# The down projection of an encoder layer as seven block products over 16 of its 22 key tiles

## The chip, the cores and the metric

The kernel runs on one core of a Trainium2 chip. The metric is the device time of one execution in microseconds. A core has TensorE (PE, matmuls, with its weight loads PEld), VectorE (DVE), ScalarE (ACT), GpSimd (POOL), SyncE (SP, which here issues nearly all transfers) and its DMA queues. Each engine takes its instructions strictly in the order of the program; between engines semaphores set the order.

## The reference

One post-norm encoder layer in float32 with 1024 tokens, 1024 features and 256 memory tokens: a token mixer (bidirectional mLSTM beside a neighbourhood attention), a cross-attention into `mem`, and a gated convolutional feed-forward part. The changed part is the last line of `conv_ffn` (D_FF is 2816, 22 tiles of 128):

```python
def conv_ffn(x, w_up, b_up, w_dw, b_dw, w_down, b_down):
    h = x @ w_up + b_up
    h = lax.conv_general_dilated(h, w_dw[:, None, :], window_strides=(1,), padding='SAME', ...
                                 feature_group_count=2 * D_FF) + b_dw
    g, u = jnp.split(h, 2, axis=-1)
    y = jax.nn.gelu(g, approximate=False) * u
    return y @ w_down + b_down
...
h = layer_norm(x, ln_in_w, ln_in_b)
h = layer_norm(DN_ALPHA * h + hybrid_mixer(h, ...), ln1_w, ln1_b)
h = layer_norm(DN_ALPHA * h + memory_xattn(h, mem, ...), ln2_w, ln2_b)
h = layer_norm(DN_ALPHA * h + conv_ffn(h, ...), ln3_w, ln3_b)
```

## The kernel before, in words

**Precision.** A product in float32 is made of three passes in float16. `split16(hi, lo, src, s)` (L202 to L204) scales a tensor by a power of two `s`: ACT writes the high part, DVE the remainder. `mm3` (L223 to L226) then issues three matmuls into one PSUM bank: high by high, high by low, low by high. `scale_of` (L185 to L191) takes the largest magnitude over a list of columns and makes the power of two; so a tensor's largest value must be known before its first split. To find it for w_down, the kernel reads the whole matrix once: `survey_down` (L1694) loads one key tile of 512 KB, and ACT takes its magnitude with a running sum into a column of `sums`.

**The stages**, in the order of the program, with the names that its tiles have in the profile: the input LayerNorm and the memory's keys and values; the token columns of the first projection (`tk`), with the cross-attention's `kv_gen` beside them; the block products of the mLSTM's q and k columns (`cu`, `units_gen`); the mLSTM chunks (`ml_gen`), between whose steps `mix` puts the remaining columns (`cl`, `col_gen`, 16 outputs of 24 matmuls each); the neighbourhood attention with the first output projection as fill; the cross-attention; the up projection in 22 units (`z`); the down projection (`dn`); the last LayerNorm. "The q/k columns" in this text are both the `cu` and the `cl` stage.

**Seven products for eight.** In the `cu` stage and in the units, a matrix product is cut into 2 x 2 blocks and done as seven block products rather than eight, with sums of blocks of the activations (`B11`, `T2`, ...) and of the weights (`A11`, `S2`, ...). In a unit, `prep` (L1549) makes the weight sums on POOL (four additions or subtractions of 128x512) and splits all on ACT and DVE; `take` (L1673) brings the banks into the tile C; `post` (L1648) does the convolution and the gate on ACT and DVE, writes the result y to memory (`y_d`, one tile of 128 channels x 1024 tokens per unit) and measures it. The other engines run at most two units ahead, since the buffers `ur` (raw weights) are two.

**The down projection** is plain. For each half of the output's columns (512 of 1024), for each of 8 token tiles, 22 key tiles x 3 passes go into one bank. y comes in pairs of tiles, is split once (`y_pair`, L1705) and stays; w_down comes in pairs too (`w_pair`, L1719), each half when it is wanted. The first 18 key tiles and the last 4 have scales of their own, because the last units end late; the two are joined by `ratio`. The first half's sums wait in `half0` (L1827 to L1855); the second half is followed tile by tile by the residual (POOL and DVE), the LayerNorm and the store (L1870 to L1889).

**What sets the order.** The program is written in the order of issue, apart from `mix` in the mLSTM stage, which lets a column product follow when the chunk has used up a given time. Generators (`kv_gen`, `units_gen`, `col_gen`, `prep`) give their steps when the surrounding loop calls them. All loads of raw weights and all stores share SP's list; a transfer whose source or target isn't ready holds everything behind it on SP. On chip, pools with a number of buffers (`bufs`) make a tile wait until the previous user of its buffer has been read for the last time.

## Time and profile before

| | us |
|---|---|
| median of the runs (3) | 1486.83 |
| lowest and highest | 1483.25, 1490.03 |
| the profiled execution, time | 1483.54 |
| the profiled execution, span | 1481.5 |
| PE busy in the span | 1432.5 (97%) |
| DVE, ACT, POOL busy | 1032.4 (70%), 820.2 (55%), 564.4 (38%) |
| moved by DMA | 208.61 MB, mean 141 GB/s |
| down projection, 1227.5 to 1474 | 246.5, of it PE 246.5 |
| q/k columns, 257 to 472 | 215, of it PE 212.2 |

How to read the lines that follow. A row of groups gives the source line, engine, operation, the tiles written and read, the shape of the first operand, the count, the busy time in all and the mean of one in ns, and the idle time of the engine just before these instructions with what ended it. A row of time order begins with the start and the duration in us; in brackets stands how long the engine had stood and for what. A row of stretches gives start and end, length, then busy time (and count) of PE, PEld, DVE, ACT and POOL, the granted TensorE clock (1.00 is full), the share of the 16 DMA engines that were busy, and GB/s.

### The profile page before, as it was taken

How to read it: one execution, taken by the hardware profiler on the slowest of the kernel's cores; microseconds unless marked ns; L12 is line 12 of the kernel's file. 1: busy time of each engine (PE TensorE's matmuls, PEld its weight loads, DVE VectorE, ACT ScalarE, POOL GpSimd, SP SyncE). 2: the span in 40 equal slices, each digit the busy share in tenths (PEclk: the TensorE clock that was granted, in tenths of full speed). 3: DMA queues.
4: the chain of work that ended last, by engine and by line, in shares of the span. 5: the costliest groups of instructions: out<-in, count | busy, mean ns of one | idle time of the engine just before them, and what ended most of it. 6: DMA issues, size and time to landing. Idle time of an engine off the chain costs nothing. (4 is left out here: it accounts for less than half of the span.)

```text
span 1481.5 us, 21508 instructions
## 1 busy us (share of the span) xinstructions
PE 1432.5 (97%) x7996; PEld 843.8 (57%) x7996; DVE 1032.4 (70%) x1946; ACT 820.2 (55%) x1385; POOL 564.4 (38%) x444
## 2 busy tenths in 40 slices
PE   8999899999999999999999799999999999999998
PEld 6998776456766777764444344444444444444444
DVE  7867866545777778588655958887778788717424
ACT  5765465564553677334546677777777866503001
POOL 5452356403324765055112534443444310300543
PEclk9999999999999999999999899999999999999999
DMA  8846654224654544743423323332333336703121
GB/s 305 311 182 196 187 197 149 79 50 136 161 146 158 199 137 155 272 128 63 99 53 114 126 90 128 128 133 108 123 132 116 136 125 237 255 29 109 48 71 58
DMA packets 116383, 208.61 MB, mean 141 GB/s; under 512 B 40627, under 2 KB 69555, under 8 KB 112950
## 3 DMA queue, kind: packets, MB, share of 16 engines
q1 hardware_dynamic: 115984, 206.47, 41.7%
q8 instruction: 63, 1.03, 0.3%
q0 software_dynamic: 144, 0.49, 0.2%
q14 instruction: 42, 0.34, 0.1%
q10 hardware_dynamic: 150, 0.27, 0.0%
HBM read 154.15 MB, written 45.15 MB: 135 GB/s over the span
## 5 line engine op out<-in xcount | busy, mean ns | idle before, releaser
L1567 POOL TENSOR_TENSOR wraw<-ur 128x512 f32<-128x512 f32 x22 | 45.8, 2082 | 205.2 <-issue 190.5
L225 PE MATMUL dn<-wlo,yp 128*128 128x512 f16 (+1 forms) x284 | 105.1, 370 | 0.0
L224 PE MATMUL dn<-whi,yp 128*128 128x512 f16 (+1 forms) x284 | 104.9, 370 | 0.0
L226 PE MATMUL dn<-whi,yp 128*128 128x512 f16 (+1 forms) x284 | 104.4, 370 | 0.0
L1655 DVE SCALAR_TENSOR_TENSOR cbuf<-C,wdw,cbuf 128x1024 f32<-128x1024 f32 x44 | 70.2, 1595 | 36.1 <-ACT cbuf L1654 36.0
L226 PEld LDWEIGHTS <-wlo 128*128 128x128 f16 x540 | 52.8, 98 | 56.5 <-DVE wlo L204 1.3
L225 PEld LDWEIGHTS <-whi 128*128 128x128 f16 x540 | 52.8, 98 | 54.7 <-issue 1.9
L224 PEld LDWEIGHTS <-whi 128*128 128x128 f16 x540 | 52.9, 98 | 53.2 <-ACT whi L203 0.3
L242 POOL TENSOR_TENSOR lnrs<-lnrs,mhalf 128x1 f32<-128x1 f32 x32 | 24.9, 777 | 133.7 <-DVE lnrs L241 96.2
L204 DVE SCALAR_TENSOR_TENSOR wlo<-wraw,us,whi 128x1024 f16<-128x1024 f32 (+1 forms) x48 | 62.7, 1323 | 18.6 <-ACT whi L203 18.6
L1656 DVE SCALAR_TENSOR_TENSOR cbuf<-C,wdw,cbuf 128x1024 f32<-128x1024 f32 x44 | 70.5, 1603 | 0.7
L252 ACT ACTIVATE r<-r,lnrs 128x1024 f32<-128x1024 f32 x19 | 23.5, 1238 | 81.4 <-DVE lnrs L251 81.3
L203 ACT ACTIVATE whi<-wraw,us 128x1024 f16<-128x1024 f32 (+1 forms) x48 | 51.1, 1102 | 15.5 <-DVE us L176 15.4
L225 PEld LDWEIGHTS <-yp 128*128 128x128 f16 x370 | 36.2, 98 | 39.9
L1654 ACT ACTIVATE cbuf<-C,bdw,wdw 128x1024 f32<-128x1024 f32 x44 | 54.2, 1234 | 8.6 <-DVE C L1692 8.1
L224 PEld LDWEIGHTS <-yp 128*128 128x128 f16 x370 | 36.2, 98 | 39.8
L226 PEld LDWEIGHTS <-yp 128*128 128x128 f16 x370 | 36.2, 98 | 39.7
L224 PE MATMUL tk<-whi,Bo 128*128 128x256 f16 (+1 forms) x192 | 52.6, 274 | 2.6 <-DVE stage L204 2.6
L225 PE MATMUL tk<-wlo,Be 128*128 128x256 f16 (+1 forms) x192 | 52.4, 274 | 0.8 <-DVE wlo L204 0.8
L224 PE MATMUL tk<-whi,Be 128*128 128x256 f16 (+1 forms) x192 | 52.5, 274 | 0.2 <-DVE stage L204 0.2
L226 PE MATMUL tk<-whi,Bo 128*128 128x256 f16 (+1 forms) x192 | 52.5, 274 | 0.0
L225 PE MATMUL tk<-wlo,Bo 128*128 128x256 f16 (+1 forms) x192 | 52.5, 274 | 0.0
(527 smaller groups left out, 4821.6 us busy)
## 6 DMA issues: line engine op xcount, KB each, us to landing
ur<-in_w_up_dram SPq DMA_DIRECT2D x22, 1024.0 KB
sv<-in_w_down_dram SPq DMA_DIRECT2D x22, 512.0 KB
y<-cbuf SPq DMA_DIRECT2D x22, 512.0 KB
ur<-y SPq DMA_DIRECT2D x11, 1024.0 KB
wraw<-in_w_down_dram SPq DMA_DIRECT2D x22, 512.0 KB
r<-h SPq DMA_DIRECT2D x11, 512.0 KB
wraw<-in_w_tok_dram SPq DMA_DIRECT2D x10, 512.0 KB
wr<-in_w_xk_dram SPq DMA_DIRECT2D x8, 512.0 KB
```

Source lines behind the costliest of these rows:

```text
L203: A.activation(hi, src, AF.Copy, scale=s)
L204: return V.scalar_tensor_tensor(lo, src, s, hi, op0=OP.mult, op1=OP.subtract)
L224: T.matmul(ps, lh, rh, start=first, stop=False, skip_group_check=skip)
L225: T.matmul(ps, lh, rl, start=False, stop=False, skip_group_check=skip)
L226: return T.matmul(ps, ll, rh, start=False, stop=last, skip_group_check=skip)
L242: G.tensor_tensor(rs[:, 0:1], rs[:, 0:1], mhalf[:, 0:1], OP.pow)
L252: A.activation(r, r, AF.Identity, scale=rs[:, 0:1], bias=rs[:, 1:2])
L1567: G.tensor_tensor(S1, A21, A22, OP.add)
L1654: A.activation(c, C[:, 1:SEQ + 1], AF.Identity, scale=wdw[:, 1, j:j + 1], bias=bdw[:, j:j + 1])
L1655: V.scalar_tensor_tensor(c, C[:, 0:SEQ], wdw[:, 0, j:j + 1], c, op0=OP.mult, op1=OP.add)
L1656: V.scalar_tensor_tensor(c, C[:, 2:SEQ + 2], wdw[:, 2, j:j + 1], c, op0=OP.mult, op1=OP.add)
```

## The change

Three parts, in the order of the program.

1. **The survey of w_down moves.** The 22 loads and ACT passes of `survey_down` leave the units and are issued in the token columns, one at each of 22 of the 32 steps, into two buffers `svd`.

2. **The weight forms are made early.** The 22 key tiles are numbered f. Of the first 16, tile i and tile i + 8 (i from 0 to 7) make a 2 x 2 block: two key halves by two column halves B11, B12, B21, B22. `wd_gen` loads both (1 MB, one buffer `draw`), and POOL makes T1 = B12 - B11, T2 = B22 - T1, T3 = B22 - B12 and T4 = B21 - T2, in place where it can. Seven forms are split (two buffers `dhl`) and stored to `wf_d`, 256 KB each. The last six key tiles are only split and stored (`wl_d`). The steps are called two at a time at each yield of `units_gen`, one at each yield of `ml_gen` (`with_prep`), and what is left runs before the attention.

3. **The down projection.** The 1024 tokens are cut by even (a = 0) and odd (a = 1) token tiles, the 16 keys into halves: A11, A12 (even), A21, A22 (odd). The seven products, each of 4 token tiles x 8 key tiles x 3 passes into four banks of 512 columns: A11·B11, A12·B21, A22·T4, S2·T2, S1·T1, S3·T3 and S4·B22, with S1 = A21 + A22, S2 = S1 - A11, S3 = A11 - A21, S4 = A12 - S2. `a_plain` reads one block's tiles of y again in rows of 512 B and splits them (128x2048); `a_sums` reads a pair of y tiles whole (1 MB) and makes S2 and S1, or S3 and S4, of it on DVE, then splits both. `b_load` reads the stored forms, on POOL's queue (the first one on SP's). `into` adds banks into the result C (128 x 8 x 1024), by a copy on ACT or an addition on DVE. The last six key tiles follow as plain products for both column halves, tile by tile, in the order of odd tiles and then even ones, and with them the LayerNorm. The scale of y now has exponent 12 rather than 14 for the first 16 tiles (sums of three blocks must fit), NG is 16, and the residual is added early, four tiles at a time (`rest`).

The arithmetic changes (sums of blocks in float32 before they are split); the result is the same function of the inputs.

```diff
@@ token columns
+                    def survey_down(i):
+
+                        t = w1.tile([128, D], F32, name="svd", tag="svd", bufs=2)
+                        S.dma_start(t, I["w_down"][i // 2, :, i % 2 * 1024:i % 2 * 1024 + 1024])
+                        A.activation(t, t, AF.Abs, accum_out=sums[:, NFF + i:NFF + i + 1])
+
                     for c in range(4):
                         w, ic = cw[2 + c]
                         for tt in range(NT):
+                            if 4 <= 8 * c + tt < 4 + NFF:
+                                survey_down(8 * c + tt - 4)
@@ q/k columns
+            FORMS = ("B11", "B21", "T4", "T2", "T1", "T3", "B22")
...
+            def wd_gen():
+
+                sd = scale_of(sums[:, NFF:2 * NFF], 12)[1]
+                scales["d"] = sd
+
+                def load(fs):
+                    raw = dp.tile([128, 2, 1024], F32, name="draw", tag="draw")
+                    for n, f in enumerate(fs):
+                        S.dma_start(raw[:, n], I["w_down"][f // 2, :, f % 2 * 1024:f % 2 * 1024 + 1024])
+                    return raw
+
+                def put(dst, src):
+                    hl = dp.tile([128, 2, 512], F16, name="dhl", tag="dhl", bufs=2)
+                    split16(hl[:, 0], hl[:, 1], src, sd)
+                    S.dma_start(dst, hl)
+
+                for i in range(8):
+                    raw = load((i, i + 8))
+                    T2 = dp.tile([128, 512], F32, name="dsum", tag="dsum")
+                    B11, B12, B21, B22 = (raw[:, a, c:c + 512] for a in range(2) for c in (0, 512))
+                    yield
+                    for n, src in enumerate((B11, B21)):
+                        put(wf_d[n, :, :, i], src)
+                        yield
+                    T1, T3, T4 = B11, B12, B21
+                    G.tensor_tensor(T1, B12, B11, OP.subtract)
+                    G.tensor_tensor(T2, B22, T1, OP.subtract)
+                    yield
+                    G.tensor_tensor(T3, B22, B12, OP.subtract)
+                    G.tensor_tensor(T4, B21, T2, OP.subtract)
+                    for n, src in enumerate((T4, T2, T1, T3, B22)):
+                        put(wf_d[2 + n, :, :, i], src)
+                        yield
+                for i in range(3):
+                    raw = load((16 + 2 * i, 17 + 2 * i))
+                    yield
+                    for n in range(2):
+                        for c in (0, 512):
+                            put(wl_d[i, :, :, n, c:c + 512], raw[:, n, c:c + 512])
+                            yield
...
             for n, _ in enumerate(units_gen(cu0)):
+                for _ in range(2):
+                    next(wd, None)
...
-            mix(tc, anchor, ml_gen(), 48.3, cg, 12, 3)
+            mix(tc, anchor, with_prep(ml_gen()), 48.3, cg, 12, 3)
+            run(wd)
@@ units
-                if v < NFF - 2:
-                    survey_down(v)
-                    if v in (0, 10):
-                        survey_down(NFF - 1 - v // 10)
@@ down projection
+            def a_plain(name, q, s):
+
+                f0, a = 8 * (name[2] == "2"), int(name[1] == "2")
+                raw = y_raw().rearrange("p (f t) -> p f t", f=4)
+                for i in range(4):
+                    S.dma_start(raw[:, i].rearrange("p (j t) -> p j t", t=128),
+                                y_d[f0 + 4 * q + i].rearrange("p (j a t) -> p a j t", a=2, t=128)[:, a])
+                t = AF_[name][:, :, 4 * q:4 * q + 4]
+                split16(t[:, 0], t[:, 1], raw, s)
+
+            def a_sums(i, names, s):
+
+                raw = y_raw().rearrange("p (f t) -> p f t", f=2)
+                for n in range(2):
+                    S.dma_start(raw[:, n], y_d[i + 8 * n])
...
+                if names[0] == "S2":
+                    V.tensor_tensor(t[:, 1], o, o8, OP.add)
+                    V.tensor_tensor(t[:, 0], t[:, 1], e, OP.subtract)
+                else:
+                    V.tensor_tensor(t[:, 0], e, o, OP.subtract)
+                    V.tensor_tensor(t[:, 1], o, o8, OP.add)
+                    V.tensor_tensor(t[:, 1], t[:, 1], e, OP.subtract)
+                    V.tensor_tensor(t[:, 1], e8, t[:, 1], OP.subtract)
+                for n, name in enumerate(names):
+                    h, l = (AF_[name][:, k, i].rearrange("p (j t) -> p j t", t=128) for k in range(2))
+                    split16(h, l, t[:, n], s)
+
+            def b_load(name, home=None):
...
+                for q in range(2):
+                    for k in range(2):
+                        (S if name == "B11" else G).dma_start(v[k][q], wf_d[n, :, k, 4 * q:4 * q + 4])
...
+            def dprod(banks, a, b, first, js=range(4), outer=False):
+                for j, i in [(j, i) for i in range(8) for j in js] if outer else [(j, i) for j in js for i in range(8)]:
+                    t = AF_[a][:, :, i, j * 128:j * 128 + 128]
+                    mm3(banks[j], t[:, 0], t[:, 1], *BF_[b][i], first and i == 0, i == 7, skip=True)
...
+            def into(banks, a, c, add):
+                for j in range(4):
+                    t = C[:, 2 * j + a, c * 512:c * 512 + 512]
+                    if add:
+                        V.tensor_tensor(t, t, banks[j], OP.add)
+                    else:
+                        A.activation(t, banks[j], AF.Copy)
...
+            into(X4, 0, 0, False)
...
+            dprod(Z4, "A12", "B21", True)
+            into(Z4, 0, 0, True)
+            for q in range(2):
+                a_plain("A22", q, s1)
...
+            dprod(Z4, "A22", "T4", True)
+            into(Z4, 1, 0, False)
...
+            for i in range(8):
+                a_sums(i, ("S2", "S1"), s1)
+            dprod(X4, "S2", "T2", False, outer=True)
+            into(X4, 0, 1, False)
...
+            dprod(W4, "S1", "T1", True, outer=True)
+            into(W4, 1, 1, False)
...
+            for i in range(8):
+                a_sums(i, ("S3", "S4"), s1)
+            dprod(X4, "S3", "T3", False, outer=True)
...
+            into(X4, 1, 0, True)
+            into(X4, 1, 1, True)
+            for n in range(4):
+                rest(n)
+            dprod(W4, "S4", "B22", False)
+            into(W4, 0, 1, True)
...
+            for tt in order:
...
+                    for f in range(NG, NFF):
```

How this moves the instructions is shown at three places.

SP's list in the mLSTM part of the q/k columns, before: `nqk` are finished columns on their way out, `mo` and `irow` the chunk's inputs, `wraw` the next column's weight.

```order
L973 DMA nqk<-ev_3963 512x1x128
L973 DMA nqk<-ev_4147 512x1x128
L928 DMA mo<-mo 128x512
L973 DMA nqk<-ev_4181 512x1x128
L946 DMA wraw<-in_w_col_dram 128x1024
```

The same place now: `dhl` is a split weight form, `wf` its place in memory, `draw` the raw pair of key tiles.

```order
L1035 DMA nqk<-ev_4265 512x1x128
L915 DMA wf<-dhl 256x1x512 x3
L909 DMA draw<-in_w_down_dram 128x1024 x2
L915 DMA wf<-dhl 256x1x512
L1035 DMA nqk<-ev_4473 512x1x128
L990 DMA mo<-mo 128x512
L915 DMA wf<-dhl 256x1x512
L1035 DMA nqk<-ev_4507 512x1x128
L915 DMA wf<-dhl 256x1x512 x2
L1008 DMA wraw<-in_w_col_dram 128x1024
```

Between two column stores stand one to three stores of forms, and a block's two loads stand behind the last form of the block before.

ACT in a middle unit, before: two evictions of C, the survey of one tile `sv`, then a gate's step (`cbuf`) and the next unit's splits.

```order
L1680 ACTIVATE C_9040<-z,bup,us 128x4x128
L1686 ACTIVATE C_9045<-z,bup,us 128x4x128
L1699 ACTIVATE sv_9039,sums<-sv_9039 128x1024
L1660 ACTIVATE cbuf<-cbuf 128x1024
L203 ACTIVATE unitA<-ur,us 128x1536
```

The same place now:

```order
L1753 ACTIVATE C_9465<-z,bup,us 128x4x128
L1747 ACTIVATE C_9466<-z,bup,us 128x4x128
L1727 ACTIVATE cbuf<-cbuf 128x1024
L1730 ACTIVATE cbuf,sums<-cbuf 128x1024
L206 ACTIVATE whi<-ur,us 128x1536
```

The instruction on `sv` is gone, and the gate's step follows the evictions directly.

DVE where the down projection follows the last gate, before: splits of w_down and y, then the copies of the first half's banks.

```order
L1661 TENSOR_TENSOR cbuf<-cbuf 128x1024
L188 TENSOR_REDUCE sc<-sums 128x1
L204 SCALAR_TENSOR_TENSOR wlo<-wraw,sc,whi 128x1024
L204 SCALAR_TENSOR_TENSOR yp<-wraw,sc,yp 128x1024
L204 SCALAR_TENSOR_TENSOR wlo<-wraw,sc,whi 128x1024 x2
L1838 COPY half_12033<-dn 128x512 x4
```

The same place now: `zw` are the banks of a product, `AA` a plain token form, `AS` a sum's form.

```order
L1728 TENSOR_TENSOR cbuf<-cbuf 128x1024
L191 TENSOR_REDUCE sc<-sums 128x1
L1919 TENSOR_TENSOR C<-C,zw 128x512 x2
L207 SCALAR_TENSOR_TENSOR AA_12396<-ur,sc,AA_12396 128x2048 x2
L1919 TENSOR_TENSOR C<-C,zw 128x512
L1790 TENSOR_TENSOR wraw<-ur 128x512
L1791 TENSOR_TENSOR wraw<-wraw,ur 128x512
L207 SCALAR_TENSOR_TENSOR AS_12636<-wraw,sc,AS_12636 128x512
```

The splits of w_down are gone from here. The split of A22 stands behind two additions of banks, and the sums behind the split.

More of the change, by code (lines that the diff above doesn't have):

```diff
@@ L1638, in encoder @@
             cbuf = xp.tile([128, 4096], F32, name="cbuf", tag="X2l").rearrange("p (i t) -> p i t", i=4)
-            sv = [vecs.tile([128, D], F32, name=f"sv{i}", tag=f"vec{i}") for i in range(2)]
             Cs = [wk.tile([128, SEQ + 2], F32, name=f"C{i}") for i in range(6)]
@@ L1714, in y_pair @@
                 for i in range(2):
[L1715 to L1716 removed]
+                    t = home[:, i]
+                    split16(t[:, 0], t[:, 1], raw[:, i], s)
                     ys[f + i] = t[:, 0], t[:, 1]
[L1719 to L1734 removed]
@@ L1736, in dmm, with w_pair @@
-            def dmm(ps, tt, c, fs, first, last, cs=slice(0, 512)):
-                t0 = slice(tt * 128, tt * 128 + 128)
-                for f in fs:
-                    wh, wl = wdn[c, f // 4]
-                    mm3(ps, ys[f][0][:, t0], ys[f][1][:, t0], wh[:, f % 4, cs], wl[:, f % 4, cs],
-                        first and f == fs[0], last and f == fs[-1])
+            def w_pair(i):
+                h, l = (wp.tile([128, 2048], F16, name=t, tag=t, bufs=5).rearrange("p (f c) -> p f c", f=2)
+                        for t in ("whi", "wlo"))
+                for n, t in enumerate((h, l)):
+                    G.dma_start(t, wl_d[i, :, n])
+                for n in range(2):
+                    wl[16 + 2 * i + n] = h[:, n], l[:, n]
@@ L1783, in encoder @@
                 if v == NFF - 1:
-                    w_pair(0, 0)
-                    y_pair(2, s1)
+                    b_load("B11", w3)
+                    a_plain("A11", 1, s1)
                 if v > 0:
@@ L1796, in encoder @@
                     posts.append(post(v - 1))
[L1797 to L1800 removed]
                 units.bound(v + 3)
             v = NFF - 1
[L1804 to L1810 removed]
+            a_home("A12", "X2h")
+            X4 = [bank("dx") for j in range(4)]
+            dprod(X4, "A11", "B11", True, range(1))
+            a_plain("A12", 0, s1)
+            dprod(X4, "A11", "B11", True, range(1, 3))
+            a_plain("A12", 1, s1)
+            b_load("B21", "Yh")
             prod(X[v], v, "A22", "T4", False, True)
@@ L1815, in encoder @@
             run(posts.pop())
-            for tt in range(5, NT):
-                ps[tt] = bank("dn")
-                dmm(ps[tt], tt, 0, range(4), True, False)
+            dprod(X4, "A11", "B11", True, range(3, 4))
             run(post(v))
@@ new lines, in encoder @@
+            b_load("B22")
+            yq = [f16(xp.tile([128, 4096], F32, name="yp", tag=t)).rearrange("p (f n t) -> p f n t", f=4, n=2)
+                  for t in ("X1l", "X1h")]
+            for i in range(3):
+                y_pair(NG + 2 * i, sy[1][1], yq[i // 2][:, i % 2 * 2:i % 2 * 2 + 2])
+            rt = xp.tile([128, 4096], F32, name="rt", tag="X2l").rearrange("p (i c) -> p i c", i=4)
+            lb = rt[:, 3]
+            S.dma_start(lb, bcast_row(I["ln3_b"], D))
+            order = [1, 3, 5, 7, 0, 2, 4, 6]
@@ new lines, in encoder @@
+            into(W4, 0, 1, True)
+            for i in range(3):
+                w_pair(i)
+            for n in range(4, 8):
+                rest(n)
+            for tt in order:
+                r = C[:, tt]
+                last = tt == order[-1]
+                for a, n in ((0, 512), (512, 256), (768, 256)) if last else ((0, 512), (512, 512)):
+                    p = bank("dn")[:, :n]
+                    for f in range(NG, NFF):
+                        t0 = slice(tt * 128, tt * 128 + 128)
+                        mm3(p, ys[f][0][:, t0], ys[f][1][:, t0], wl[f][0][:, a:a + n], wl[f][1][:, a:a + n], f == NG,
+                            f == NFF - 1)
+                    V.scalar_tensor_tensor(r[:, a:a + n], p, ratio, r[:, a:a + n], op0=OP.mult, op1=OP.add)
```

167 lines of the change are left out of this document (68 added, 99 removed).

## The prediction

> **What bounds the kernel now.** I read the page first, then the busy time of each engine by stage, then who waited for whom, then single stretches in order of time.
>
> ```profile
> span 1481.5 us, 21508 instructions
> ...
> PE 1432.5 (97%) x7996; PEld 843.8 (57%) x7996; DVE 1032.4 (70%) x1946; ACT 820.2 (55%) x1385; POOL 564.4 (38%) x444
> ...
> GB/s 305 311 182 196 187 197 149 79 50 136 161 146 158 199 137 155 272 128 63 99 53 114 126 90 128 128 133 108 123 132 116 136 125 237 255 29 109 48 71 58
> ```
>
> TensorE is busy 1432.5 of 1481.5 us: 49 us of gaps are all that better waiting could win, and matmuls taken away come off the time one for one, as long as new gaps don't open. The highest of the 40 slices moves 311 GB/s. By stage (columns: stretch, its length, busy time of PE, PEld, DVE, ACT, POOL with counts, granted clock, DMA share, GB/s):
>
> ```profile
> 120.00:257.00 137.00, 131.65 (x1086) 106.03 (x1084) 100.22 (x197) 77.09 (x134) 68.25 (x88) 1.00 0.56 181
> 257.00:335.00 78.00, 76.12 (x394) 40.18 (x393) 38.17 (x92) 48.49 (x104) 19.50 (x16) 1.00 0.23 66
> 335.00:472.00 137.00, 136.04 (x843) 90.46 (x842) 93.30 (x336) 70.42 (x181) 43.23 (x42) 1.00 0.53 148
> 472.00:655.00 183.00, 173.45 (x1008) 134.09 (x1007) 138.93 (x377) 101.66 (x276) 98.30 (x94) 0.99 0.54 179
> ...
> 852.00:950.00 98.00, 91.40 (x424) 40.81 (x422) 75.06 (x85) 73.25 (x86) 44.66 (x25) 1.00 0.32 120
> 950.00:1227.50 277.50, 275.79 (x1289) 125.36 (x1287) 222.31 (x269) 207.12 (x241) 103.32 (x54) 1.00 0.33 125
> 1227.50:1474.00 246.50, 246.50 (x1198) 117.05 (x1196) 126.12 (x149) 64.42 (x64) 61.46 (x30) 1.00 0.33 114
> 1474.00:1481.50 7.50, 0.20 (x2) 0.00 (x0) 3.97 (x8) 0.00 (x0) 0.92 (x1) 0.85 0.18 70
> ```
>
> In this order they are the token columns, the q/k columns (block products to 335, then the mLSTM chunks with the other columns beside them), the neighbourhood attention, the first up-projection units, the other units, the down projection, and the last LayerNorm. The q/k columns and the down projection have no gap to speak of, so a new wait there shows in full; DVE works 68% of the mLSTM part.
>
> **Part 1, matmuls removed.** A row of time order per size of output gives the price: starts are 1302.31 - 1299.72 = 2.59 us apart over twelve matmuls of 512 columns, 0.216 each, and 1466.07 - 1462.90 = 3.17 over twenty-nine of 256, 0.109 each.
>
> ```profile
> 1299.72 0.38 PE L225 MATMUL dn<-wlo,yp 128*128 128x512 f16 x1
> ...
> 1302.31 0.38 PE L225 MATMUL dn<-wlo,yp 128*128 128x512 f16 x1
> 1462.90 0.27 PE L224 MATMUL dn<-whi,yp 128*128 128x256 f16 x1
> ...
> 1466.07 0.27 PE L226 MATMUL dn<-whi,yp 128*128 128x256 f16 x1
> L225 PE MATMUL dn<-wlo,yp 128*128 128x512 f16 (+1 forms) x284 | 105.1, 370 | 0.0
> L225 PE MATMUL dn<-ur,yp 128*128 128x512 f16 x58 | 22.0, 379 | 0.0
> L225 PE MATMUL dn<-yp 128*128 128x512 f16 x16 | 6.1, 379 | 0.0
> ```
>
> Before, the code issues 1002 matmuls of 512 and 108 of 256 (the last tile's second half is cut in two). Now seven products of 4 token tiles x 8 key tiles x 3 passes make 672, and six plain key tiles 270 of 512 and 36 of 256. That is 60 x 0.216 + 72 x 0.109 = **20.8 us less**. A product of 96 takes 20.7 us.
>
> **Part 2, the survey of w_down leaves the units.** ACT measures 22 pieces there, and stands before the transfer of each:
>
> ```profile
> L1699 ACT ACTIVATE sv<-sv 128x1024 f32<-128x1024 f32 x22 | 23.2, 1054 | 41.3 <-DMA sv<-in_w_down_dram 41.3
> 863.10 1.06 ACT L1699 ACTIVATE sv<-sv 128x1024 f32<-128x1024 f32 x1 [3.84 <-DMA sv<-in_w_down_dram]
> 868.51 0.38 PE L224 MATMUL z<-TX1h,unitYh 128*128 128x512 f16 x1 [1.98 <-ACT C L1686]
> ```
>
> ACT stands 3.84 us, its next evictions of C come late, and PE waits 1.98. PE's gaps in the units are 6.6 + 1.7 = 8.3 us. Not all follow a survey, and the gate behind ACT may only move to DVE, which is busy 80% from 950 on. Bounds 0 and -8; I take **-4**, half.
>
> **Part 3, the same survey in the token columns.** 22 x 1.05 us more make ACT 100 of 137 us; 11.5 MB over some 95 us put 121 GB/s on top of 181, just under 311. Its cover is PSUM, six banks ahead of ACT and DVE. If a transfer is late, ACT stands, and behind it stand the splits of w_xq and w_xo, then the kv products. Bounds 0 and 6 (the stands of 3.84, with a few reaching PE); I take **+1.5**.
>
> **Part 4, the weight forms in the q/k columns.** Added: 68 splits of 128x512 (ACT and DVE one each), 32 POOL subtractions of that size, 22 loads of 512 KB, 68 stores of 256 KB. The prices, in one unit's preparation:
>
> ```profile
> 262.28 1.27 POOL L475 TENSOR_TENSOR hm<-wraw 128x512 f32<-128x512 f32 x1
> 264.18 0.71 ACT L203 ACTIVATE whi<-ev,us 128x512 f16<-128x512 f32 x1
> 265.25 16.38 SPq L456 DMA_DIRECT2D wraw<-in_w_cu_dram  x4
> 265.31 2.13 POOL L477 TENSOR_TENSOR hm<-wraw,ev 128x512 f32<-128x512 f32 x1
> 266.23 2.42 DVE L204 SCALAR_TENSOR_TENSOR wlo<-ev,us,whi 128x512 f16<-128x512 f32 x2
> 268.57 1.40 DVE L204 SCALAR_TENSOR_TENSOR wlo<-hm,us,whi 128x512 f16<-128x512 f32 x2
> 272.45 1.06 ACT L308 ACTIVATE whi<-wraw 128x1024 bf16<-128x1024 f32 x1 [1.69 <-DMA wraw<-in_w_cu_dram]
> ```
>
> A DVE split takes 0.70 us alone and 1.21 while POOL works; a POOL subtraction 1.27 alone and 2.13 beside DVE. Some 64 splits lie in these 215 us. DVE goes from 38.2 + 93.3 = 131.5 to 176 (at 0.70) or 209 (at 1.21); ACT from 118.9 to 164; POOL from 62.7 to 103 or 131; DMA by 29.4 MB from 118 to some 250 GB/s. Nothing passes 215, but DVE is left 6 to 39 us of the 83 in which it stood before, and most of those were waits for others' results in a fixed order. With 0.95, the middle, 22 us are left; if half of the old 83 must stay, 19.5 us are missing. The bounds are 0 and 20; I take **+8**, since the cover is PE's own backlog of column matmuls, 384 of them, which waits for none of this.
>
> [...]
>
> The queues: a store waits for DVE's split, and behind it on SP stand the loads of the next column weight, of the gate rows and of the next raw block. POOL's subtractions stand before the masks and powers of the mLSTM chunks. The attention after it starts behind the last four stores, and has less column work left as cover: -2 to +6, I take **+1**.
>
> **Part 5, the down projection's supply.** Now y is read three times. From the end of A11·B11 (call it zero) until the last key tile of S3·T3 is wanted, 4 x 20.7 + 18 = 101 us later, there must land 2 MB for A22, 16 for the sums and 9 of weight forms: 27 MB, 267 GB/s. This stage's own busiest stretch:
>
> ```profile
> 1250.00:1300.00 50.00, 50.00 (x234) 22.66 (x232) 36.74 (x28) 25.29 (x26) 12.17 (x4) 1.00 0.70 241
> L204 DVE SCALAR_TENSOR_TENSOR yp<-ur,sc,yp 128x1024 f16<-128x1024 f32 x18 | 22.3, 1279 | 3.3 <-ACT yp L203 3.3
> L1838 DVE COPY half<-dn 128x512 f32<-128x512 f32 x8 | 5.5, 690 | 33.7 <-PE dn L226 33.6
> L1044 DVE TENSOR_TENSOR hm<-hm,mo 128x512 f32<-128x512 f32 x8 | 6.1, 767 | 4.0 <-ACT hm L1043 4.0
> ```
>
> At 241 GB/s 27 MB take 112 us, 11 too many; at 311, 87. DVE: A22 5.1, eight S2/S1 blocks of 2 x 0.77 + 2 x 0.70 = 23.5, eight S3/S4 blocks of 4 x 0.77 + 2 x 0.70 = 35.7, sixteen additions of 0.69, six y splits of 1.28: 83 of 104 us. The tightest place is A22, whose split stands on DVE behind two additions that wait for half of A12·B21: 10.4 + 1.4 + 5.1 = 16.9, wanted at 20.7. S2/S1 blocks then come every 3.4 to 4.4 us (1 MB each), the last by 17 + 35 + 3 = 55, wanted at 59.5. So the forms are in time, with 4 us to spare twice. Bounds 0 and 11; I take **+2**. The weight forms come on POOL's queue, which has nothing else to do then. The last 7.5 us stay: the same LayerNorm behind a final 256-column piece.
>
> **Sum.** 1481.5 - 20.8 - 4 + 1.5 + 8 + 1 + 2 = 1469.2 of span. The profiled execution took 1483.5, 2.0 more than its span: 1471.2. The runs shown have their median 3.3 above that execution and one as low; I predict **1472 us**.
>
> **Rivals.**
> *The form chain sets the pace of the q/k columns (slower).* One raw buffer serves all blocks, so a block is serial: two loads (265.25 to the end of ACT's wait at 272.45: 7.2 us), a split 1.4, four subtractions 5.1 to 8.5, and five splits through two buffers, each (0.71 + 0.70 + a store)/2. A 256 KB store isn't seen; half of a load pair's 7.2 is the nearest, so 2.5 each. A block takes 26 to 30 us, eight 209 to 237, and three plain ones of 17 make 51: 260 to 288 us for a stretch of 215. Every engine takes its queue in order, so what isn't absorbed by the attention's start is PE's gap. With 32 us in place of 8 the time is 1496; it decides from 29 us on, where all gains are gone. For it: the single buffer. Against: the order spreads the steps over the whole stretch and lets the last run into the attention, where PE has 192 matmuls of fill.
> *Everything is covered.* Parts 3 to 5 cost nothing and the units give 7: 1481.5 - 20.8 - 7 + 2 = 1456, or 1459 by the median. For it: PE's backlog and 30% of idle DVE; against: DVE's 88% in the columns.
> *The sums starve the products.* At 241 GB/s part 5 costs 11: 1481.
>
> **How the numbers follow.** Forecast 0.47 (own range 1463 to 1480), form chain 0.17, all covered 0.15, starved sums 0.17, anything else 0.04. What a measurement here can tell from no change is about 0.5%, so faster means under 1479 and slower over 1494. Faster: 0.43 of the forecast, 0.15, and 0.04 of the starved: 0.62. Slower: 0.14 of the chain and 0.02: 0.16. Same: 0.22. The range 1459 to 1495 leaves out half of the chain's case and the better half of the covered one.
>
> **What would show it.** Part 1: the stretch from the last unit to the last matmul is about 19 us shorter with PE without gaps. Part 2: PE's gaps in the units fall from 8.3 towards 4. Part 4: the q/k columns grow by some 8 us, with PE waiting for DVE; gaps before col weights or masks that SP's stores or POOL hold would speak for the chain. Part 5: no PE wait for AS or AA tiles; such waits, at DMA shares over 0.8, are the starved case. I am wrong if the columns grow by over 20 us, or the down projection keeps its length.

## The result, and the profile after

The changed kernel takes 1549.92 us (median of 4 runs, 1547.98 to 1552.14), the kernel before 1487.18: 1.0424 times as long, 95% interval 1.0394 to 1.0454. The forecast was 1472, in a range of 1459 to 1495. The rows below come from the two profiled executions, 1483.54 and 1551.66 us, which lie 68 us apart; the medians lie 63 apart. The page of the changed kernel:

```profile
span 1549.9 us, 21849 instructions
...
PE 1442.0 (93%) x7864; PEld 838.1 (54%) x7864; DVE 1120.9 (72%) x2062; ACT 867.0 (56%) x1469; POOL 620.8 (40%) x502
```

To compare stages, both traces are cut at the same places: the first matmul of `cu`, of `cl`, of the attention's `fill`, of the cross-attention, of `z`, of the down projection, and after the last matmul. First the kernel before, without its first 253.0 us (columns as in the rows of stretches above; the cross-attention, 171.1 us, is left out):

```profile
253.00:336.10 83.10, 81.22 (x423) 43.14 (x422) 43.27 (x99) 51.65 (x110) 20.57 (x17) 1.00 0.25 75
336.10:470.20 134.10, 133.14 (x823) 87.85 (x821) 91.39 (x335) 69.94 (x180) 42.72 (x40) 1.00 0.54 150
470.20:651.30 181.10, 171.55 (x1001) 133.93 (x1000) 137.78 (x374) 100.02 (x274) 96.75 (x93) 0.99 0.52 174
...
822.40:1227.60 405.20, 388.61 (x1805) 176.15 (x1804) 326.20 (x392) 300.19 (x358) 167.10 (x101) 0.99 0.34 126
1227.60:1473.90 246.30, 246.30 (x1196) 117.03 (x1195) 126.02 (x148) 64.32 (x64) 61.46 (x30) 1.00 0.33 114
1473.90:1481.50 7.60, 0.30 (x3) 0.01 (x1) 3.97 (x8) 0.00 (x0) 0.92 (x1) 0.85 0.18 69
```

The changed kernel, which begins its `cu` stage at 257.7:

```profile
257.70:366.00 108.30, 92.71 (x445) 46.76 (x444) 66.64 (x136) 69.64 (x144) 44.40 (x34) 0.92 0.50 159
366.00:525.80 159.80, 139.19 (x804) 87.92 (x802) 114.03 (x360) 88.62 (x203) 62.75 (x55) 0.95 0.69 207
525.80:734.20 208.40, 179.17 (x1001) 137.27 (x1000) 142.96 (x384) 107.07 (x286) 97.27 (x93) 0.93 0.54 177
734.20:906.30 172.10, 171.24 (x819) 80.50 (x819) 116.86 (x225) 84.10 (x174) 50.80 (x32) 1.00 0.37 91
906.30:1314.90 408.60, 398.00 (x1852) 180.63 (x1851) 338.48 (x392) 286.29 (x320) 166.13 (x103) 0.99 0.30 106
1314.90:1539.60 224.70, 219.48 (x1016) 99.64 (x1015) 149.34 (x186) 58.68 (x74) 72.84 (x53) 0.98 0.54 199
1539.60:1549.90 10.30, 0.31 (x3) 0.03 (x1) 6.63 (x13) 0.24 (x1) 3.27 (x2) 0.63 0.27 106
```

The differences are +4.7 to the end of the token columns, +25.2 in `cu`, +25.7 in `cl`, +27.3 in the attention, +1.0 in the cross-attention, and, from the first `z` matmul to the end, 643.6 in place of 659.1, -15.5. In sum 68.4, which is 1549.9 - 1481.5. So the feed-forward part did become shorter, and the three stages in and behind which the weight forms are made became 78.2 us longer (476.5 against 398.3). Of the 78.2, PE stands 65.4 us there in place of 12.4, 53 more, and is busy 411.1 in place of 385.9, 25 more for the same matmuls: the granted clock is 0.92, 0.95 and 0.93 in place of 1.00, 1.00 and 0.99.

One place shows how. ACT in order of time in the changed kernel, and PE's stretches of 6 us at the same place:

```profile
265.02 1.00 ACT L506 ACTIVATE k<-cu,bsc,us 128x256 f32<-128x256 f32 x2
272.05 0.72 ACT L206 ACTIVATE dhl<-draw,sc 128x512 f16<-128x512 f32 x1 [6.02 <-DMA draw<-in_w_down_dram]
273.24 0.72 ACT L206 ACTIVATE dhl<-draw,sc 128x512 f16<-128x512 f32 x1 [0.47 <-DMA draw<-in_w_down_dram]
273.86 1.75 ACT L206 ACTIVATE whi<-wraw,us 128x512 f16<-128x512 f32 x2
```

```profile
264.00:270.00 6.00, 4.76 (x23) 2.37 (x24) 3.07 (x11) 2.02 (x5) 5.22 (x6) 1.00 0.55 128
270.00:276.00 6.00, 1.50 (x5) 0.13 (x2) 3.10 (x6) 3.49 (x5) 3.22 (x3) 0.71 0.58 222
276.00:282.00 6.00, 4.82 (x12) 1.79 (x13) 6.00 (x5) 4.27 (x9) 4.45 (x3) 0.50 0.58 194
```

ACT stands 6.02 us for the raw block of w_down. Behind that instruction on ACT's list stands the split of the next q/k unit's own weight (`whi<-wraw`), for which PE waits. PE stands 4.15 us for it, up to 274.62, and in the six us from 276 on the clock granted is 0.50: PE's matmuls of 512 columns, which started 0.22 us apart before the stand, start 0.43 apart from 277.58 to 282.70, and 0.22 apart again from 282.95 on.

The groups of the form splits, with what ended the idle time before them:

```profile
L207 DVE SCALAR_TENSOR_TENSOR dhl<-draw,sc,dhl 128x512 f16<-128x512 f32 x60 | 50.0, 841 | 65.3 <-ACT dhl L206 65.1
L206 ACT ACTIVATE dhl<-draw,sc 128x512 f16<-128x512 f32 x60 | 42.6, 719 | 79.1 <-DMA draw<-in_w_down_dram 34.0 <-DMA wf<-dhl 18.7 <-POOL draw L930 13.5
```

Two rows of PE's waits, the first of the `cu` stage, the second of the attention (in all, times, longest):

```profile
PE cu L227 <- ACT whi L206: 7.4, 2, 4.2
...
PE S L227 <- ACT qsh L1275: 18.1, 1, 18.1
```

A split costs DVE 0.84 us and ACT 0.72, as priced. But ACT stood 79 us in front of them. The 18.1 in the last row is the attention's first product: its `qsh` stands on ACT's list behind the splits of the last three pairs (the last of them began at 552.3, PE's product at 555.7).

### The profile page after: what moved, and what is told of

It reads as the page before. It is cut to its first block, busy times and chain, and to the rows that moved or that the text cites. A ratio compares the mean times of both kernels' runs of the same rounds, so it can differ in the third digit from the quotient of the medians.

```text
span 1549.9 us, 21849 instructions
## 1 busy us (share of the span) xinstructions
PE 1442.0 (93%) x7864; PEld 838.1 (54%) x7864; DVE 1120.9 (72%) x2062; ACT 867.0 (56%) x1469; POOL 620.8 (40%) x502
## 5 line engine op out<-in xcount | busy, mean ns | idle before, releaser
L207 DVE SCALAR_TENSOR_TENSOR dhl<-draw,sc,dhl 128x512 f16<-128x512 f32 x60 | 50.0, 841 | 65.3 <-ACT dhl L206 65.1
L206 ACT ACTIVATE dhl<-draw,sc 128x512 f16<-128x512 f32 x60 | 42.6, 719 | 79.1 <-DMA draw<-in_w_down_dram 34.0
L1721 ACT ACTIVATE cbuf<-C,bdw,wdw 128x1024 f32<-128x1024 f32 x44 | 54.4, 1236 | 41.4 <-DVE C L1759 41.0
L206 ACT ACTIVATE AS<-wraw,sc 128x512 f16<-128x512 f32 x32 | 22.7, 720 | 69.3 <-DVE wraw L1790 30.1
L227 PE MATMUL tk<-whi,Be 128*128 128x256 f16 (+1 forms) x192 | 52.6, 274 | 0.0
L229 PE MATMUL tk<-whi,Be 128*128 128x256 f16 (+1 forms) x192 | 52.6, 274 | 0.0
L229 PE MATMUL S<-kq,h1T 128*128 128x512 f16 x128 | 48.6, 380 | 0.0
L227 PE MATMUL S<-kq,h1T 128*128 128x512 f16 x128 | 48.6, 379 | 0.0
L228 PE MATMUL S<-kq,h1T 128*128 128x512 f16 x128 | 48.6, 379 | 0.0
```

What stands on the lines that cost most here:

```text
L206: A.activation(hi, src, AF.Copy, scale=s)
L207: return V.scalar_tensor_tensor(lo, src, s, hi, op0=OP.mult, op1=OP.subtract)
L227: T.matmul(ps, lh, rh, start=first, stop=False, skip_group_check=skip)
L228: T.matmul(ps, lh, rl, start=False, stop=False, skip_group_check=skip)
L229: return T.matmul(ps, ll, rh, start=False, stop=last, skip_group_check=skip)
L1721: A.activation(c, C[:, 1:SEQ + 1], AF.Identity, scale=wdw[:, 1, j:j + 1], bias=bdw[:, j:j + 1])
```

## The experiments

Single executions differ by some us in their first 260 us alone (the token columns ended at 255.5 to 263.1 us in twelve traces that have the survey there), so most verdicts go by the length of `cu`, `cl` and attention together: 398.3 before, 476.5 after.

**1. No forms in the q/k columns.**

```diff
 def wd_gen():
     sd = scale_of(sums[:, NFF:2 * NFF], 12)[1]
     scales["d"] = sd
-    def load(fs):
...
+    yield
...
-G.dma_start(t[:, k], wf_d[n, :, k])
+G.dma_start(t[:, k], wfv[k, :, 0:8])          # another float16 tensor
```

> The changed kernel, but no weight form is made in the q/k columns; the seven products and the plain key tiles read other float16 data of the same size from memory, so the result is not the reference's. The survey stays in the token columns. Comparing the two traces, the q/k columns grew by 51 us and the attention by 27, everything else together fell by 10. If the forms alone cost this, the time is 1550 - 78 = 1472 (span 1470 to 1474), the stretch from the first cu to the first fill matmul is 217 +- 2 us and the attention 181 +- 2. If the survey, or the seven products' own traffic, has a part in it, the time is over 1482.

Measured: 1471.35 us. The three stages, and the down projection:

```profile
256.90:339.40 82.50, 81.32 (x424) 43.30 (x422) 43.42 (x101) 50.22 (x107) 21.18 (x17) 1.00 0.23 74
339.40:473.90 134.50, 133.42 (x824) 87.89 (x823) 92.39 (x335) 70.05 (x180) 43.46 (x40) 1.00 0.53 148
473.90:655.70 181.80, 171.34 (x1000) 132.64 (x998) 136.38 (x375) 100.11 (x274) 95.87 (x93) 1.00 0.52 174
...
1236.20:1458.60 222.40, 217.61 (x1017) 99.04 (x1015) 148.72 (x186) 58.10 (x74) 72.93 (x53) 0.99 0.54 200
```

Together 398.8. Without the forms, with their loads and stores, all of the 78 us are gone; the rest of the change is worth 14 (1485.28 for the kernel before, measured beside it).

**2. Column blocks of 256, a load ahead, five form buffers.**

```diff
-raw = dp.tile([128, 2, 1024], F32, name="draw", tag="draw")
+raw = dp.tile([128, 2, 2, 256], F32, name="draw", tag="draw", bufs=2)
...
-hl = dp.tile([128, 2, 512], F16, name="dhl", tag="dhl", bufs=2)
+hl = dp.tile([128, 2, 256], F16, name="dhl", tag="dhl", bufs=5)
...
+nxt = load(b + 1)                             # a block ahead
-for n, src in enumerate((T4, T2, T1, T3, B22)):
+for n, src in ((6, B22), (4, T1), (3, T2), (5, T3), (2, T4)):
```

> The changed kernel with the forms made in column blocks of 256 rather than 512: two raw buffers and a load that is issued a whole block ahead, five form buffers rather than two, and the raw forms (B11, B21, B22) split before the sums. Same bytes, twice as many and half as large splits (136 of 128x256). Theory A, chain: ACT stands in order for a block's loads (21 us), for a store to free its form buffer (19) and for POOL (14), and with it DVE and PE; with the lead these stands fall under 10 us and the q/k columns with the attention come down by at least 40 of their 78 us: time 1500 to 1515. Theory B, capacity: DVE, ACT and POOL have no room for this work beside the columns, whatever the order; smaller instructions only add to it: 1550 to 1575.

Since there are twice as many splits, this run also takes three steps at each yield of `units_gen` in place of two, and two at each of `ml_gen` in place of one.

Measured: 1530.48 us. The stages take 99.9 + 169.0 + 181.2 = 450.1: 26 of the 78 come back, the attention's all (the last split begins at 483.0, 49 us before the attention), and 52 stay. Theory A was half right, and B was wrong in that order matters. But the run doesn't take the chain away: ACT's stands for loads fell from 34 to 9.6 us, but those for stores only from 24.7 to 20.5, and those for POOL rose from 13.5 to 18.2. In all it stood 48.5 us in front of the splits, in place of 79.

**3. The last three pairs left out.**

```diff
-for i in range(3):
-    raw = load((16 + 2 * i, 17 + 2 * i))
...
```

> The changed kernel without the last three pairs' forms (six key tiles, 12 splits and stores); the plain products read other float16 data, so the result is not the reference's. In the changed kernel ACT stands for two of these loads (6.2 and 7.1 us) just ahead of the attention's first q, and PE then waits 18.1 us for it. If that is the attention's 27 us, it comes back to 181 +- 3 and the time is 1520 to 1526; the q/k columns keep their 51 us. If the blocks before are late anyway and only shift, the attention stays over 195.

Measured: 1525.23 us; the attention takes 186.8, the three stages 450.4. So 21.6 of the attention's 27.3 us are these 12 splits, which reach into it, and not a late mLSTM; 5.7 stay, a little more than the 181 +- 3 allowed.

**4. The store of a form one step later** (on top of 2).

```diff
 def put(dst, src):
+    flush()                                   # S.dma_start of the form before
     hl = dp.tile([128, 2, 256], F16, name="dhl", tag="dhl", bufs=5)
     split16(hl[:, 0], hl[:, 1], src, sd)
-    S.dma_start(dst, hl)
+    held.append((dst, hl))
```

> The run with column blocks of 256 and a load ahead, and one more edit: the store of a form is issued one step later, just before the next form's split, so that SP no longer waits for DVE's split of it (54 us of SP's waits there) with the loads of the column weights and the gate rows queued behind. That run took 1530, of which the q/k columns are still 52 us longer than before the change. If SP's queue is what is left, the columns lose at least 20 us: time 1500 to 1512. If what is left is the time of the added instructions in the queues of ACT and DVE, ahead of the mLSTM's and the columns' own steps, it stays at 1524 to 1535.

Measured: 1529.98 us, the stages 452.6: no difference in sum. (By stage they are 100.9 + 145.7 + 206.0, but here the attention's first `fill` matmul comes earlier, with 683 matmuls in `cl` in place of 820, so only the sum can be compared; run 8 has the same shift.) The edit did less than was meant. SP's waits for DVE's splits fell from 54.6 to 34.8 us only, and since a store that is issued later frees its buffer later, ACT's stands for stores of forms grew from 20.5 to 39.8. So the run exchanged one wait for another, and doesn't show what SP's queue alone costs.

**5. Without DVE's halves** (on top of 2).

```diff
-split16(hl[:, 0], hl[:, 1], src, sd)
+A.activation(hls[0][:, 0], src, AF.Copy, scale=sd)
```

> The run with column blocks of 256 and a load ahead, without DVE's half of each split: only the high parts of the forms are made, and the low parts are stored as zeros, so the result is less accurate. All loads, stores, POOL's sums and ACT's halves stay. It takes 136 instructions of 0.48 us, 65 us, off DVE, and a store waits for ACT alone. If DVE's time and its order are what the columns lack, the 52 us fall to under 20: time under 1500. If ACT's stands for loads, stores and POOL, or SP's queue, are enough, they stay over 35: 1513 or more.

Measured: 1518.17 us, the stages 446.7, 3.4 less than in 2; most of the rest of the difference in time is the first 260 us. DVE's 65 us of instructions were not the bound; ACT still stood 41 us in front of its own halves, 38 of them for transfers.

**6. Without POOL's sums** (on top of 2).

```diff
-G.tensor_tensor(T1, B12, B11, OP.subtract)
-G.tensor_tensor(T2, B22, T1, OP.subtract)
-G.tensor_tensor(T3, B22, B12, OP.subtract)
-G.tensor_tensor(T4, B21, T2, OP.subtract)
```

> The run with column blocks of 256 and a load ahead, without POOL's subtractions: the raw blocks are split in place of T1 to T4, so the result is not the reference's. ACT's and DVE's 136 halves, the loads and the stores stay. That run took 1530, 52 us over the columns before. If POOL's sums (64 of 0.73 to 0.90 us, in ACT's way and against DVE) carry much of it, the time falls by 20 us or more, under 1510. If ACT's and DVE's own instructions do, it stays over 1518.

Measured: 1518.68 us, the stages 445.7, 4.4 less than in 2. The time fell between the two ranges. With the sums gone ACT still stood 43 us in front of the splits, nearly all of it for loads and stores, so the stages came down little.

**7. Transfers only** (on top of 2).

```diff
-split16(hl[:, 0], hl[:, 1], src, sd)
-G.tensor_tensor(T1, B12, B11, OP.subtract)
...
-S.dma_start(dst, hl)
+S.dma_start(dst, hls[0])
```

> The run with column blocks of 256 and a load ahead, reduced to its transfers: the blocks are loaded and as many form tiles are stored, at the same steps, but ACT, DVE and POOL do nothing for them, and the stored forms are zeros; so the result lacks the seven products' part. Without DVE's halves the q/k columns and the attention were 48 us longer than before the change (446.7 against 398.3). If DMA traffic or SP's queue is behind that, at least 25 us of it stay: time over 1495. If it is ACT's instructions, their stands and POOL's sums, it is under 10: time 1472 to 1482.

Measured: 1519.65 us, the stages 444.2. That looks like a verdict for the transfers, but it isn't one: with no split to wait for, SP issued them in a burst, and `cu` moved 250 GB/s (159 in the changed kernel). In `cu` and `cl` together ACT waited 18.2 us for the units' own weights and 50.1 for gate rows, waits that are 2.8 and 6.0 in the changed kernel. What the run shows is that the 29 MB without pace do nearly as much harm (45.9 us) as the whole work of run 2 (51.8), by another way.

**8. Compute only**, at the changed kernel's own places.

```diff
 def load(fs):
-    raw = dp.tile([128, 2, 1024], F32, name="draw", tag="draw")
...
-    return raw
+    return raw0                               # one block, loaded once
...
-    S.dma_start(dst, hl)
```

> The changed kernel with all 68 splits and 32 subtractions in the q/k columns at their places, but on one block that stays in memory on the chip: no load of a further block and no store of a form (the products read other float16 data, so the result is not the reference's). The changed kernel's cu, cl and attention stages took 108.3 + 159.8 + 208.4 = 476.5 us against 398.3 before. If the engines' own time (57 us of DVE, 49 of ACT, POOL's sums) makes the columns long, at least 50 of the 78 us stay: time over 1520. If the chain through loads and stores does, with ACT standing for them, under 25 stay: time under 1497.

**9. The chain only**: all loads, stores and waits, with each split and sum cut to 8 of 512 columns.

```diff
-split16(hl[:, 0], hl[:, 1], src, sd)
+split16(hls[0][:, 0, :8], hls[0][:, 1, :8], src[:, :8], sd)
-G.tensor_tensor(T1, B12, B11, OP.subtract)
+G.tensor_tensor(T1[:, :8], B12[:, :8], B11[:, :8], OP.subtract)
```

> The changed kernel with all loads and stores of the forms in the same chain, but each split and each subtraction cut to 8 of 512 columns (the rest of the stored forms is zero, so the result is not the reference's): the waits stay, the engines' time goes. If the chain through loads and stores makes the columns long, at least 50 of the 78 us stay: time over 1520. If the engines' own time does, under 25 stay: time under 1497. If both this run and the one with compute only keep 40 or more, either is enough by itself.

Measured: compute only 1511.23 us, the stages 105.4 + 123.5 + 205.6 = 434.5; chain only 1536.27 us, the stages 105.8 + 165.2 + 184.0 = 455.0. ACT's splits in the two, compute only first:

```profile
L206 ACT ACTIVATE dhl<-draw,sc 128x512 f16<-128x512 f32 x60 | 42.1, 719 | 32.1 <-POOL draw L930 14.8 <-DVE dhl L207 10.6 <-DMA draw<-in_w_down_dram 6.7
```

```profile
L206 ACT ACTIVATE dhl<-draw,sc 128x8 f16<-128x8 f32 x60 | 17.5, 298 | 83.4 <-DMA draw<-in_w_down_dram 43.9 <-DMA wf<-dhl 24.1 <-issue 5.3
```

The chain alone costs 56.7 of the 78.2: 68 splits of little length, but ACT stands 83 us in front of them, mostly for their loads and stores. Compute alone costs 36.2 with hardly a transfer, and there too ACT stands 32 us in front of the splits, for POOL, for DVE and for the one load. Together they would be 93, so 15 us of them overlap. Compute only ended between its two ranges; the chain is the larger share, not the only one.

Run 9 keeps all the traffic of the forms, so it isn't the waits by themselves. But in `cu` and `cl` ACT stands only 28.2 us for the stage's own loads there, 20.9 in the kernel before, against 73.8 for the forms' loads and stores: ACT is held by the chain and not by the other transfers. Whether the traffic also makes the forms' own transfers longer, no run here separates.

ACT's stands in front of the form splits, summed over the trace, beside what the three stages take above 398.3:

| | ACT's stands, us | the stages, us more |
|---|---|---|
| changed kernel | 78.9 | 78.2 |
| run 2 | 48.5 | 51.8 |
| run 3 | 53.0 | 52.1 |
| run 4 | 52.7 | 54.3 |
| run 5 | 41.4 | 48.4 |
| run 6 | 43.3 | 47.4 |
| run 8 | 32.1 | 36.2 |
| run 9 | 84.6 | 56.7 |

In the first seven rows the two are within 7 us of each other, whatever was left out; run 9, whose splits are short, costs less than it stands, and run 7, which has no split, costs 45.9 in its own way. That is why leaving out DVE's halves or POOL's sums (5 and 6) gave so little: ACT's stands hardly fell. The rows go together; they don't prove that the stands are all of the cost.

**10. The residual rows on POOL, later.** In the changed kernel S3·T3 lies in a stretch of 30 us in which PE is busy 24.78 (a product takes 20.7):

```profile
1426.50:1456.50 30.00, 24.78 (x97) 9.66 (x96) 24.71 (x38) 11.78 (x18) 1.06 (x2) 0.89 0.73 252
```

Some 20 us ahead of it DVE begins with the sums for S3. POOL, then DVE, in order of time:

```profile
1405.68 2.36 POOL L1979 TENSOR_TENSOR rt<-rt,vec 128x1024 f32<-128x1024 f32 x1
...
1416.03 2.36 POOL L1980 TENSOR_TENSOR rt<-rt,vec 128x1024 f32<-128x1024 f32 x1
1418.32 0.58 POOL L1836 DMA_DIRECT2D wlo<-wl  x1
```

```profile
1405.93 13.02 DVE L1793 TENSOR_TENSOR wraw<-ur 128x512 f32<-128x512 f32 x1 [3.55 <-DMA ur<-y]
1418.87 0.68 DVE L1794 TENSOR_TENSOR wraw<-ur 128x512 f32<-128x512 f32 x1
```

```diff
-rt = xp.tile([128, 4096], F32, name="rt", tag="X2l").rearrange("p (i c) -> p i c", i=4)
+rt = yp.tile([128, 4096], F32, name="rt", tag="Yl").rearrange("p (i c) -> p i c", i=4)   # free only behind S3*T3
```

> The changed kernel with one edit: the buffer of the residual rows is the one that S3 leaves, so POOL's multiplications and additions for them start behind S3*T3 and no longer run beside the first sum of S3. In the changed kernel one DVE instruction there (128x512, else 0.69 us) took 13.02 us, exactly while POOL worked from 1405.7 to 1418.4. If POOL's work holds DVE, that instruction is back under 2 us, S3*T3 takes 21 us rather than 30, and the part up to the first dn matmul is 7 to 9 us shorter; the last LayerNorm may give some of it back, since POOL is then late by 10 to 15 us. If the 13 us have another cause (the read of y), the stretch stays at 30.

Measured: 1551.32 us; its down projection and tail:

```profile
1319.40:1534.60 215.20, 215.20 (x1017) 99.27 (x1015) 141.28 (x179) 57.80 (x73) 72.94 (x51) 1.00 0.56 205
1534.60:1549.60 15.00, 0.25 (x3) 0.00 (x0) 10.16 (x21) 1.24 (x1) 6.16 (x4) 0.59 0.27 107
```

The longest of the eight instructions of that line is 0.69 us now, the products run without a gap, and the stage is 9.5 us shorter; the tail gives back 4.7. So POOL's back-to-back work held DVE. (The time as a whole is no lower: in this execution the token columns ended 3.4 us later, and the other stages together took 1.1 more.) In the changed kernel PE waited in that stretch for the sums of S3:

```profile
PE dx L227 <- ACT AS L206: 3.9, 2, 2.6
PE dx L229 <- DVE AS L207: 1.2, 3, 0.5
```

In the traces of runs 1, 2, 3, 8 and 9, which leave this part as it is, PE waits 4.4 to 7.4 us for the sums of S3; in this run it waits for none.

**11. The survey alone**, moved in the kernel before.

```diff
 for tt in range(NT):
+    if 4 <= 8 * c + tt < 4 + NFF:
+        survey_down(8 * c + tt - 4)
...
-survey_down(v)
```

> The kernel before, with the survey of w_down moved from the units to the token columns and nothing else. In the trace without forms the token columns ended 3.9 us later than before the change and PE's gaps in the units were 5.1 us smaller. So the sum should be between -3 and +2 us: 1483 to 1488, no difference that can be told. The forecast had -4 and +1.5, -2.5 in all. If the units gain the full 8 that the bounds allowed, it is under 1481; if the token columns lose 6 or more, over 1488.

Measured: 1484.90 us against 1485.93, ratio 0.9992 (0.9979 to 1.0006): no difference that can be told.

**12. and 13. Two other homes for the work.** In the first, POOL makes the four sums in the units, out of the tiles that the survey loads there anyway; in the second, beside the cross-attention, in 16 KB per partition that are free there. Both store them in float32, add nothing to the q/k columns, and do all splits in the down projection.

The lines that stand for the change, from the first:

```diff
-split16(hl[:, 0], hl[:, 1], src, sd)                            # q/k columns
-S.dma_start(dst, hl)
+S.dma_start(wf_d[n, :, b], t)                                   # float32, a sum of POOL
...
-(S if name == "B11" else G).dma_start(v[k][q], wf_d[n, :, k, 4 * q:4 * q + 4])
+(S if name == "B11" else G).dma_start(raw, src)                 # down projection
+split16(h, l, raw, sd)
```

> Seven products, but nothing is made in the q/k columns and the survey stays in the units. There, of each pair of key tiles that the survey has loaded anyway, POOL makes T1 to T4 in float32 (four subtractions per two units, stored as 2 KB rows, 8.4 MB in all). All seven forms and the six plain key tiles are split in the down projection, 34 more splits of 128x1024 on ACT (1.1 us) and DVE (1.28): DVE goes there from 149 to some 193 of 222 us, less the 13 us stand if POOL's residual work is held behind the last forms. Expected if DVE's idle time there can be used: q/k columns and attention as before the change (398 us), units 405 to 412, down projection with its tail 228 to 240: span 1460 to 1475, time 1462 to 1477. If POOL's sums hold DVE in the units (80% busy), these grow by up to 15; if DVE's order makes the products wait, the down projection returns to 250: then 1485 or more.

> Seven products, with nothing added to the q/k columns or to the units: the survey stays in the units; POOL makes T1 to T4 in float32 beside the cross-attention (POOL busy 52 of 171 us there, DVE 116), in 16 KB per partition that are free there, one store of 1 MB per block; all splits are in the down projection. The residual rows come behind S3*T3 and then one tile ahead of each LayerNorm. From the stages of the runs so far: 253 to 257 to the end of the token columns, 398 for the q/k columns and the attention, 171 to 180 for the cross-attention, 405 to 414 for the units, 216 to 230 for the down projection, 8 to 12 for the tail: span 1455 to 1490, most likely 1470, time 1472. If POOL's sums hold DVE and the products beside the cross-attention as they did in the units (26 us for 32 sums), it is 1490 or more.

Measured: 1509.22 us, 1.0149 times the kernel before (1.0122 to 1.0175), and 1506.41 us, 1.0146 times (1.0125 to 1.0167), both outside the range that was hoped for. In the first, two stretches of a unit's length, with the sums and after them:

```profile
909.20:927.60 18.40, 14.16 (x65) 6.12 (x64) 18.10 (x10) 13.39 (x17) 18.32 (x10) 1.00 0.51 186
...
1019.60:1038.00 18.40, 18.40 (x87) 8.23 (x86) 15.33 (x18) 13.23 (x14) 7.96 (x4) 1.00 0.18 65
```

POOL is busy 18.3 of 18.4 us and DVE counts 18.1 for ten instructions in place of 15.3 for eighteen: the units took 437.2 us, 408.6 in the changed kernel. In the second, 20 of the 32 sums ran in the attention (196.5 us, +15) and the rest in the cross-attention (177.9, +7); its down projection with all splits took 247.6 with its tail, against 235.0 in the changed kernel. Neither beats the kernel before, and no version with all the forms made does.

## Why the prediction was wrong, point by point

**Part 1 was right.** From the first `z` matmul to the last, PE is busy 388.6 + 246.3 = 634.9 us before and 398.4 + 215.2 = 613.6 in run 10, where the products have no gap: 21.3 less, forecast 20.8.

**Parts 2 and 3 were right in sum, and each too small.** PE's gaps in the units went from 16.6 to 10.6 us, 6.0 less where 4 was taken (in the stretch that the working used, from 8.3 to 2.3). The token columns became 3 to 10 us longer in the twelve traces, 6 on average, where 1.5 was taken with a bound of 6. Run 11 finds the sum of both within -3.1 and +0.9; the forecast of -2.5 lies inside, and so does no change at all.

**Part 4 was the error: 8 us taken for the q/k columns with bounds 0 and 20, 50.9 measured; with the attention behind them 9 taken, 78.2 measured.** Its prices held: DVE's split 0.84 (0.70 to 1.21, taken 0.95), ACT's 0.72, POOL's sum 1.27 to 1.53 (1.27 to 2.13). Two steps failed. The first is the bound: it came from adding busy times and asking whether DVE's idle time suffices. No engine's sum set the columns' length, but how long a step stands in a queue: ACT was busy only 64% of the `cu` stage, and a split that waits there for a load or a store holds the next q/k weight, the next eviction and the attention's first q behind it. Run 9 shows 57 us with the chain and hardly any instruction time, run 8 36 with the instructions and hardly a transfer. The second is the cover that was named, "PE's own backlog of column matmuls, which waits for none of this": in `cu` there is no such backlog (PE stood 15.6 us in it, 7.4 of them for the units' weights that ACT splits), and the columns' own weights are split by the same ACT behind the forms.

**The rival of the form chain had the right mechanism and length, and too small a price.** It put the chain at 260 to 288 us; from the first split (272.05) to the last it took 281. But it charged only what runs over the stretch's end, 32 us, a figure for which the working gives no sum (260 to 288 run over 215 by 45 to 73); and by the forecast's own terms the gains are gone at 20 us for part 4, not at 29. Run 3 shows 26 us for the last pairs, at the end; the other 52 lie all along the stretch, where ACT's stands become gaps of PE. On top came what was not in the sum at all, the granted clock after a gap (0.50 after the stand of 4.15 us): 25 of the 78 us are longer matmuls. The chance of 0.17 was too low for a single buffer with a serial chain on an engine that is in everybody's way; and the range, which "leaves out half of the chain's case", was cut on the side where nothing in the working bounded the cost.

**The attention's +1** (bounds -2 to 6) was 27.3: the row of the order showed the last stores in front of the attention, and the working charged the stores, not ACT's splits in front of `qsh`.

**Part 5, 2 taken, some 12 measured**: 9.5 in the stage and 2.7 in the tail. The rival of the starved sums named the right tiles and the wrong reason. PE did wait 5.1 us for the sums of S3, but their stretch had 0.73 of the DMA, and S2·T2, two products earlier, ran without a gap at the highest DMA share of the stage:

```profile
1385.00:1405.70 20.70, 20.70 (x97) 9.38 (x96) 10.43 (x15) 6.36 (x10) 4.57 (x6) 1.00 1.01 384
```

No product waited for A22 or S2, as the working said. What was missed is the residual on POOL, which the working named nowhere beside the sums; run 10, with POOL's work later, has no gap.

Without part 4 and the attention's +1, the sum's other terms give 1481.5 - 20.8 - 4 + 1.5 + 2 = 1460.2, and run 1 measured a span of 1469.6: 9.4 us off: 2.4 in the token columns, 6.5 from the units to the end.

## What to carry to other kernels

Here the work that was moved under another stage cost above all what it made the in-order queues wait, and the sum of busy times didn't show that (ACT stood 79 us for 48 us of added instructions): for each added instruction, ask what it waits for (a load into a single buffer, a store that frees one) and which of the stage's own instructions stands behind it on that engine. In stages where PE had hardly a gap (12.4 us in 398.3), such stands became gaps, and the gaps were paid a second time in the clock (53 us more of them came with 25 us of longer matmuls, at 0.92 to 0.95). And when one cause after another is left out, look whether the wait that it stood for is gone, too: in runs 4 to 6 it wasn't. A saving of 21 us on PE does not carry 68 splits and 32 sums in a kernel whose DVE is 70% busy: in all three places that were tried, they cost more than that.

## What was not expected of the hardware

One DVE instruction with two inputs, 0.69 us long by itself, took 13.02 while POOL did five multiplications and additions of 128x1024 and two DMA issues in a row (run 10 took POOL's work away and it was 0.69 again). It began 0.25 us after the first of POOL's five and ended, at 1418.95, 0.56 us after the last of them. The rows that the prediction used had 1.21 us in place of 0.70 for a DVE split beside POOL's work.

The chain with hardly any instruction time (56.7 us) and the instructions with hardly a transfer (36.2) add up to more than both together (78.2), and transfers without their pace cost 46.
